# A two-layer encoder trunk: the pre-norm root moved to the product's eviction, the residual taken through PSUM chunk by chunk, and the other half's steps placed in the chains at a fixed pace

## Chip, cores and metric

The kernel runs on one NeuronCore of a Trainium2 chip. The metric is the device time of one execution in microseconds: three runs gave 1231.95, 1235.25 and 1236.02 us, median 1235.25 us. The trace quoted below comes from one further execution under the hardware profiler, which took 1234.75 us.

## What is computed

The reference is a trunk of two layers on one sequence of 512 positions with 1024 channels, in float32. Every sub-layer is a sandwich of two RMS norms around a function f:

```python
def rms_norm(x, g):
    y = x * lax.rsqrt(jnp.mean(x * x, axis=-1, keepdims=True) + EPS)
    return y * g

for i in range(2):
    g = sandwich_gains[i]
    h = rms_norm(x, g[0])
    m = parallel_conv_mla(h, ...) if i == 0 else conformer_conv(h, ...)
    x = x + rms_norm(m, g[1])
    h = rms_norm(x, g[2])
    x = x + rms_norm(jnp.square(jax.nn.relu(h @ w1[i])) @ w2[i], g[3])
```

Layer 0's mixer is a gated short convolution beside latent attention, followed by one output projection (`wout`). Layer 1's mixer is a Conformer module: a projection to 2048 columns (`pw1`) with a GLU (a times the sigmoid of g), a depthwise convolution of 31 taps, a LayerNorm over the channels, SiLU, and a projection (`pw2`). The MLP has 4096 hidden columns.

What matters for the change is that an RMS norm is a gain per channel times one factor per position, the reciprocal root of the mean square. The factor is the same for all channels of a position, so it can be applied to `h` before a matrix product or to the product's columns after it.

## The kernel before

**Layout.** Channels lie on the 128 partitions and positions along the free axis, so a 1024-channel activation is 8 tiles, called chunks here (`xs`, `ms`, `hs`). Every float32 operand of a matrix product is split into a high and a low part, and a product is three matmuls (`mm`, lines 252 to 254): high by high, high by low, low by high. A step is one output block of 128 channels over 8 input chunks, 24 matmuls. ScalarE (ACT) writes the high half as a rounded copy, VectorE (DVE) or GpSimd (POOL) subtracts it to get the low half (`split`, lines 236, 239 and 242). Weights come in by DMA in strips, are split in the same way (`strip`, lines 228 to 230) and are prepared some strips ahead (`take`).

**Halves and steps.** The positions are worked in two halves, A and B, each 256 wide (240 and 272 in layer 1). `M0`, `M2` and `M3` list tokens, and `run` turns them into steps. The tokens `up`, `down`, `pw1`, `pw2` and `wout` are products: eight steps to a group. `up` is a block of `w1` with the squared ReLU (written to `hid`); `down` is a block of `w2`, added to `m`; `pw1` makes two products and the GLU, and then starts the convolution of that channel chunk. The tokens `join`, `norm` and `finish` are chains: work on one half that PE can do little for.

**The chains.** A `join` ends one sub-layer and prepares the next: `residual` takes the reciprocal root of the mean square of `m` (`rstds`: a sum over partitions with matmuls at line 345, a Newton iteration of twelve small DVE operations at lines 376 to 407, and a spreading matmul at line 417), multiplies each chunk of `m` by it (446) and adds it, with the gain, to `x` in place (439). `prenorm` squares the new `x` chunk by chunk on ACT (336), adds the squares on DVE (323), takes the second root in the same way, and then makes each chunk of `h` = x times gain times root (465) and its two halves (236, 239). Only then can the next product of that half begin. `norm` is the LayerNorm of the Conformer module (`layer_norm`, 818 to 831). `finish` writes the output.

**What sets the order.** In `M2` and `M3` the DVE instructions run in the order in which the program emits them (`manual_schedule`); the scheduler orders the other engines by its own estimates, and in `M0` DVE too. Each engine's queue is in order. While a half is in a chain, `pull(i)` at fixed places of the chain emits some of the following steps of the other half; how many is listed by hand for each chain in `PULLS`, or else in `PULL`. So for `join A 1 1` the tuple (2, 2, 0, 0, 9) means two steps before the first root, two after it, none before and after the squares, and nine after the second root.

**The convolution.** Its 31 taps a chunk are DVE operations on a PSUM bank (786), emitted between the product steps: each step grants a number of microseconds (`FILL`), and one tap is emitted for every 0.4 us (`TAP_US`). `norm` first emits the taps that are left.

**PSUM.** There are eight banks: three `S`, two `pj`, one `o`, two `mi`. Products take `S` and `pj` in turn, but `S` alone while convolutions, which live in `pj`, are open (`accum`). Scratch tiles of the chains take `o` and `mi`.

**An up step's eviction** is `y` = Relu of the product on ACT (480), its square on ACT (482), or on DVE for the four tokens in `SQ` (484), the high half on ACT (236) and the low half on DVE (242).

Of the kernel before, what the change touches and what calls it, by code (L numbers as in the profile page):

```python
# [42 lines left out]
FILL = {'up': 2.2, 'down': 3.2, 'first': 2.7, 'sum': 0, 'pw1': 3.9, 'pw2': 2.8, 'last': 5.1, 'wout': 1.5}  # L43
# [17 lines left out]
CHAIN = {"sq": 3, "acc1": 2, "t": 2, "t2": 2}  # L61
# [73 lines left out]
def trunk(ctx: ExitStack, tc: tile.TileContext, a, out: bass.AP):  # L135
# [15 lines left out]
    def phase(name, acc, **tags):  # L151

        pool = tc.tile_pool(name=name, bufs=1, reuse_waits="tile")
        scope.update(name=name, sb=pool.__enter__(), tags=tags, acc=acc, turn=0, scr=0, scratch=["o", "mi"], raws=0, los=0, lo=(1, 0), sum=nc.vector)
        return pool
# [19 lines left out]
    def scratch(w):  # L177


        scope["scr"] += 1  # L180
        return ps(scope["scratch"][scope["scr"] % len(scope["scratch"])])[:, :w]
# [115 lines left out]
    def pull(i):  # L297

        scope["pulling"] = True
        n = scope["pulls"][i]  # L300
        while n and steps and not steps[0][0] and steps[0][1][1] not in ("F", scope["half"]):
            steps.pop(0)[2]()
            n -= 1
        scope["pulling"] = False
# [127 lines left out]
    def residual(xs, ms, s, gain, seg):  # L432

        pull(0)
        bc = rstds(s, "post")
        pull(1)

        def add(j, t):
            nc.vector.scalar_tensor_tensor(
                out=xs[j][seg.sl], in0=t, scalar=col(gain + j), in1=xs[j][seg.sl],  # L440
                op0=ALU.mult, op1=ALU.add,
            )

        for j in range(NC):
            t = scratch(seg.w)
            nc.vector.tensor_tensor(out=t, in0=ms[j][seg.sl], in1=bc, op=ALU.mult)
            settle()
            late.append(lambda j=j, t=t: add(j, t))
        settle()

    def prenorm(xs, gain, hs, seg):

        hs = views(hs, seg)
        s = Sum(NC, seg, whole=WHOLE[0])
        pull(2)
        for j in range(NC):
            s.square(xs[j][seg.sl])
            settle(1)
        settle()
        pull(3)  # L460
        bc = rstds(s, "pre")
        pull(4)
        for j in range(NC):
            t = scratch(seg.w)
            nc.vector.scalar_tensor_tensor(
                out=t, in0=xs[j][seg.sl], scalar=col(gain + j), in1=bc, op0=ALU.mult, op1=ALU.mult
            )
            settle()
            split((hs[j][0][seg.sl], hs[j][1][seg.sl]), t, nc.vector, late=late)
        settle()  # L470
# [4 lines left out]
    def up(w, hs, dst, seg):  # L475
# [4 lines left out]
        nc.scalar.activation(y, acc, AF.Relu)  # L480
        if scope["square"] is nc.scalar:
            nc.scalar.activation(acc, y, AF.Square)
        else:
            nc.vector.scalar_tensor_tensor(
                out=acc, in0=acc, scalar=0.0, in1=y, op0=ALU.max, op1=ALU.mult
            )
        split((dst[0][cols], dst[1][cols]), acc, nc.vector)
# [266 lines left out]
    def glu(c, wa, wg, seg):  # L754
# [3 lines left out]
        tg = tmp("sg")[:, : seg.w]  # L758
        nc.scalar.activation(tg, accg, AF.Sigmoid, bias=col(V_BPW1 + NC + c))
# [33 lines left out]
    def layer_norm(seg):  # L793
# [15 lines left out]
        pull(0)  # L809
        s2 = Sum(NC, seg, whole=WHOLE[2])  # L810
        for c in range(NC):
# [8 lines left out]
            s2.square(v)  # L820
        settle()
        pull(1)
        rb = rstds(s2, "var")
        pull(2)
        for c in range(NC):
# [5 lines left out]
            split((hv[c][0][seg.sl], hv[c][1][seg.sl]), t, nc.vector, late=late)  # L831
        settle()
# [10 lines left out]
    hid, sums, kept, us = {}, {}, {}, []  # L843
# [4 lines left out]
    def up_step(tok, h, layer, g, m):  # L848
# [3 lines left out]
        scope["square"] = nc.vector if tok[:4] in SQ else nc.scalar  # L852
        up(take(), hs, hid[h][m], seg)
        fill(FILL["up"])

    def down_step(tok, h, layer, g, m):
        last = g == G - 1
        if last and m == 0:
            sums[h] = Sum(NC, seg_of(h, layer), whole=WHOLE[4])
# [15 lines left out]
    def pw1_step(tok, h, c):  # L875
        seg = seg_of(h, 0)
        glu(c, take(), take(), seg)
# [22 lines left out]
    def join_step(tok, h, layer, n):  # L900
        seg = seg_of(h, layer)
        residual(xs, ms, sums[h], gains(layer, n), seg)
        prenorm(xs, gains(layer, 2) if n == 1 else gains(layer + 1, 0), hs, seg)

    def finish_step(tok, h):
        seg = seg_of(h, 1)
        pull(0)
        bc = rstds(sums[h], "finish")
        pull(1)
# [12 lines left out]
        for j in (*pool, *(j for j in range(NC) if j not in pool)):  # L922
# [5 lines left out]
            late.append(lambda j=j, x=x, t=t: add(j, x, t))  # L928
        settle()

    def run(program, in_order=True):
# [38 lines left out]
        with order:  # L970
            while steps:
                chain, tok, fn = steps.pop(0)
                if chain:
# [138 lines left out]
```

## Time and profile before

| | |
|---|---|
| median of three runs | 1235.25 us |
| the profiled execution's own time | 1234.75 us |
| its span, first to last instruction | 1232.9 us |
| mean granted clock of TensorE | 0.977 |
| weights and inputs read from HBM | 180.42 MB, 148 GB/s over the span |
| share of the chain that ended last | PE 81%, DVE 12%, ACT 3% |

The time lies 1.85 us above the span. Some first readings: the page gives each engine's busy time with its share of the span and its number of instructions, then 40 slices of 30.8 us each, one digit a slice, in tenths. PE's busy time is modelled: matmuls overlap, so a matmul of 256 columns shows as 0.28 us although the next one starts 0.12 us later. Counts in a window tell more than busy time. A line "X <- Y: a, b, c" in the list of waits means that X waited for Y for a us in all, b times, c us at the longest. A row of a timeline has the start in us, the duration in us, the engine, the line of the kernel and the tiles; a wait before it stands in brackets at its end.

### The profile page before, as it was taken

The page shows a single profiled execution, that of the slowest core. Times are in us where ns is not written, and L with a number is a line of the kernel's source. Part 1 is how long each engine was busy: PE and PEld are TensorE (multiplying, and loading weights), DVE is VectorE, ACT ScalarE, POOL GpSimd, SP SyncE. Part 2 cuts the span into 40 slices and gives each one's busy share as a digit, 9 for nine tenths or more (in the row PEclk, how much of TensorE's full clock was granted, in tenths as well). Part 3 has the DMA queues.
Part 4 walks back from the last instruction along what each step waited for, and adds up shares of the span by engine and source line. Part 5 has one row for each costly group of instructions (what it writes and reads, how often), then busy time and mean ns, then how long its engine had stood idle before and what let it go on. Part 6 is the DMA issues. An engine that isn't in the chain of part 4 may idle for free.

```text
span 1232.9 us, 22940 instructions
## 1 busy us (share of the span) xinstructions
PE 1176.0 (95%) x8926; PEld 1131.6 (92%) x8926; DVE 706.3 (57%) x1667; ACT 660.0 (54%) x1174; POOL 787.6 (64%) x388
## 2 busy tenths in 40 slices
PE   6999989999999999999999989999999889999996
PEld 3788869989999999899999989999999889999996
DVE  7843599555254235678965547498995354261313
ACT  4421577455555556546466746564455756445462
POOL 5564563145857777688874644688886665748680
PEclk9999999999999999999998989899999899999998
DMA  6331232044644565455543524655552652636341
GB/s 202 110 100 35 90 112 69 1 154 138 226 155 137 206 231 184 149 185 190 180 160 127 202 90 171 206 189 188 171 173 85 222 171 86 217 124 222 124 152 37
DMA packets 55405, 184.01 MB, mean 149 GB/s; under 512 B 6400, under 2 KB 10880, under 8 KB 55296
## 3 DMA queue, kind: packets, MB, share of 16 engines
q1 hardware_dynamic: 54864, 182.00, 44.1%
q8 instruction: 70, 1.15, 0.4%
q10 hardware_dynamic: 432, 0.54, 0.1%
q14 instruction: 39, 0.32, 0.1%
HBM read 180.42 MB, written 2.10 MB: 148 GB/s over the span
## 4 chain that ended last, share of the span: by engine, by line
PE 81%; DVE 12%; ACT 3%; issue 1%; DMA 1%; POOL 0%; SPq 0%; DVEq 0%; ACTq 0%
PE S L252 17%; PE S L253 17%; PE S L254 17%; PE pj L252 8%; PE pj L253 8%; PE pj L254 8%; DVE pj L786 4%; PE mi L345 1%; PE mi L417 1%; ACT whi L229 1%; DVE ycat L323 1%; DVE pr L721 1%; DVE h L535 1%; PE mi L724 1%; DVE s L715 1%
## 5 line engine op out<-in xcount | busy, mean ns | idle before, releaser
L230 POOL TENSOR_TENSOR wlo<-raw,whi 128x1024 fp32r<-128x1024 f32 (+3 forms) x316 | 738.1, 2350 | 374.9 <-ACT whi L229 348.9
L229 ACT ACTIVATE whi<-raw 128x1024 fp32r<-128x1024 f32 (+2 forms) x347 | 355.7, 1031 | 408.2 <-PE S L253 169.9
L252 PE MATMUL S<-h,whi 128*128 128x256 f32 (+2 forms) x1120 | 328.7, 295 | 8.9 <-ACT h L236 3.9
L253 PE MATMUL S<-h,whi 128*128 128x256 f32 (+2 forms) x1120 | 328.9, 294 | 0.1
L254 PE MATMUL S<-h,wlo 128*128 128x256 f32 (+2 forms) x1120 | 327.6, 293 | 0.0
L252 PEld LDWEIGHTS S<-h,whi 128*128 128x128 f32 x1120 | 213.1, 191 | 15.0 <-ACT h L236 4.7
L253 PEld LDWEIGHTS S<-h,whi 128*128 128x128 f32 x1120 | 213.6, 191 | 4.9 <-DVE h L239 1.3
L254 PEld LDWEIGHTS S<-h,wlo 128*128 128x128 f32 x1120 | 213.8, 191 | 3.6
L254 PE MATMUL S<-hid,wlo 128*128 128x256 f32 (+1 forms) x680 | 194.4, 286 | 0.0
L253 PE MATMUL S<-hid,whi 128*128 128x256 f32 (+1 forms) x680 | 194.0, 286 | 0.0
L786 DVE SCALAR_TENSOR_TENSOR pj<-u,taps,pj 128x240 f32<-128x240 f32 (+1 forms) x464 | 192.4, 489 | 1.1
L252 PE MATMUL S<-hid,whi 128*128 128x256 f32 (+1 forms) x680 | 192.4, 285 | 0.5 <-DVE m L494 0.5
L252 PE MATMUL pj<-h,whi 128*128 128x256 f32 (+2 forms) x432 | 132.6, 307 | 10.6 <-ACT whi L229 4.8
L253 PE MATMUL pj<-h,whi 128*128 128x256 f32 (+2 forms) x432 | 132.5, 307 | 2.6 <-DVE h L536 2.6
L254 PE MATMUL pj<-h,wlo 128*128 128x256 f32 (+2 forms) x432 | 130.6, 302 | 0.0
L252 PEld LDWEIGHTS S<-hid,whi 128*128 128x128 f32 x680 | 129.7, 191 | 0.8 <-DVE m L494 0.7
L254 PEld LDWEIGHTS S<-hid,wlo 128*128 128x128 f32 x680 | 130.2, 192 | 0.1
L253 PEld LDWEIGHTS S<-hid,whi 128*128 128x128 f32 x680 | 129.9, 191 | 0.0
L253 PE MATMUL pj<-hid,whi 128*128 128x256 f32 (+1 forms) x344 | 100.4, 292 | 0.0
L254 PE MATMUL pj<-hid,wlo 128*128 128x256 f32 (+1 forms) x344 | 99.7, 290 | 0.0
L252 PE MATMUL pj<-hid,whi 128*128 128x256 f32 (+1 forms) x344 | 98.9, 289 | 0.0
L252 PEld LDWEIGHTS pj<-h,whi 128*128 128x128 f32 x432 | 82.5, 191 | 16.2 <-ACT whi L229 7.6
(214 smaller groups left out, 1854.7 us busy)
## 6 DMA issues: line engine op xcount, KB each, us to landing
raw<-in_w SPq DMA_DIRECT2D x256, 512.0 KB, 3.8
raw<-in_pw SPq DMA_DIRECT2D x48, 512.0 KB, 3.6
raw<-in_win SPq DMA_DIRECT2D x16, 512.0 KB, 3.4
x<-in_xT SPq DMA_DIRECT2D x16, 256.0 KB, 4.2
raw<-in_wout SPq DMA_DIRECT2D x8, 512.0 KB, 3.4
raw<-in_wq SPq DMA_DIRECT2D x8, 192.0 KB, 2.3
out<-x SPq DMA_DIRECT2D x8, 120.0 KB, 1.7
out<-x SPq DMA_DIRECT2D x6, 136.0 KB, 1.8
```

The source lines that it names most:

```text
L229: nc.scalar.activation(h, r, AF.Copy)
L230: eng.tensor_tensor(out=lo[:, c0:c1], in0=r, in1=h.bitcast(F32), op=ALU.subtract)
L252: nc.tensor.matmul(acc, sh, mh, start=i == 0, stop=False)
L253: nc.tensor.matmul(acc, sh, ml, start=False, stop=False)
L254: nc.tensor.matmul(acc, sl, mh, start=False, stop=i == n - 1)
L323: self.eng.tensor_tensor(out=dst, in0=acc, in1=t, op=ALU.add)
L345: nc.tensor.matmul(s[:bw, b : b + 1], q[:, cols], one, start=i == 0, stop=i == len(self.parts) - 1,)
L417: nc.tensor.matmul(o[:, sl], r[:, b : b + 1].to_broadcast([bw, P]), ident[:bw, :bw], start=True, stop=True,)
L535: nc.vector.tensor_scalar(out=hi, in0=x, scalar1=g, scalar2=None, op0=ALU.mult)
L715: nc.vector.reduce_max(out=mx, in_=S, axis=AX.X)
L721: eng.tensor_scalar(out=pr_, in0=pr_, scalar1=sm, scalar2=None, op0=ALU.mult)
L786: nc.vector.scalar_tensor_tensor(out=dst, in0=src, scalar=wk, in1=acc, op0=ALU.mult, op1=ALU.add)
```

## The change

Five things are edited together.

- `join` replaces `residual` and `prenorm`. After the first root, a loop over the chunks makes three things per chunk, one turn apart: the product with the root into a PSUM scratch tile, the new residual into another PSUM scratch tile, and from that the two halves of `h` = x times gain (without a root) and the copy of the residual back to `x` on ACT. Then come the squares, the second root, and a copy of its spread to a tile `bcs` of its own for each half.
- `up` and `glu` apply that root where the product is evicted: `up` on DVE, as max(product, 0) times root, in place of the Relu on ACT, with the square always on ACT and the low half emitted one step later; `glu` by two more DVE operations per step. `SQ` goes.
- `pull` and its tables go. `pace(us)` adds an estimated time and emits one step of the other half whenever 2.9 us have gathered.
- In a chain, the steps that are emitted take `S` banks alone, and scratch tiles turn through `o`, `pj`, `mi`, `pj`.
- `FILL` for `up` falls from 2.2 to 1.9 us.

```diff
-PULLS = {('join', 'B', 0, 1): (3, 8, 4, 4, 7), ('join', 'A', 0, 1): (0, 0, 1, 4, 2), ('finish', 'B'): (0, 31), ('join', 'B', 0, 3): (1, 5, 0, 5, 5), ('norm', 'B'): (0, 2, 2), ('finish', 'A'): (3, 4), ('join', 'A', 0, 3): (0, 2, 1, 3, 5), ('norm', 'A'): (0, 0, 5), ('join', 'A', 1, 1): (2, 2, 0, 0, 9), ('join', 'B', 1, 1): (0, 1, 0, 3, 1)}
-PULL = {'join': (0, 1, 2, 0, 1), 'norm': (0, 2, 1), 'finish': (0, 2)}
-SQ = {('up', 'B', 1, 0): 1, ('up', 'A', 0, 2): 1, ('up', 'A', 0, 0): 1, ('up', 'B', 1, 1): 1}
+STEP_US, EDGE_US, ROOT_US, CHUNK_US, SQUARE_US = 2.9, 1.0, 2.8, 1.45, 0.5
...
-FILL = {'up': 2.2, 'down': 3.2, 'first': 2.7, 'sum': 0, 'pw1': 3.9, 'pw2': 2.8, 'last': 5.1, 'wout': 1.5}
+FILL = {'up': 1.9, 'down': 3.2, 'first': 2.7, 'sum': 0, 'pw1': 3.9, 'pw2': 2.8, 'last': 5.1, 'wout': 1.5}
...
-        tags = [t for t in scope["acc"] if t != "pj" or not (convs or todo)]
+        tags = [t for t in scope["acc"] if t != "pj" or not (convs or todo or scope.get("chain"))]
...
+        tags = ["o", "pj", "mi", "pj"] if scope.get("chain") else ["o", "mi"]
+        return ps(tags[scope["scr"] % len(tags)])[:, :w]
...
+    def pace(us):
+        scope["time"] += us
+        while scope["time"] >= STEP_US and steps and not steps[0][0] and steps[0][1][1] not in ("F", scope["half"]):
+            scope["time"] -= STEP_US
+            scope["pulling"] = True
             steps.pop(0)[2]()
+            scope["pulling"] = False
+        scope["time"] = min(scope["time"], STEP_US)
...
+    def join(xs, ms, s, post, pre, hs, seg, h):
+        hv = views(hs, seg)
+        pace(EDGE_US)
         bc = rstds(s, "post")
+        pace(EDGE_US + ROOT_US)
+        ts, xn = {}, {}
+        for j in range(NC + 2):
+            if j < NC:
+                ts[j] = scratch(seg.w)
+                nc.vector.tensor_tensor(out=ts[j], in0=ms[j][seg.sl], in1=bc, op=ALU.mult)
+            if 1 <= j <= NC:
+                i = j - 1
+                xn[i] = scratch(seg.w)
+                nc.vector.scalar_tensor_tensor(
+                    out=xn[i], in0=ts[i], scalar=col(post + i), in1=xs[i][seg.sl], op0=ALU.mult, op1=ALU.add
+                )
+                nc.scalar.activation(hv[i][0][seg.sl], xn[i], AF.Copy, scale=col(pre + i))
+                nc.scalar.activation(xs[i][seg.sl], xn[i], AF.Copy)
+            if j >= 2:
+                i = j - 2
+                nc.vector.scalar_tensor_tensor(
+                    out=hv[i][1][seg.sl], in0=xn[i], scalar=col(pre + i), in1=hv[i][0][seg.sl].bitcast(F32),
+                    op0=ALU.mult, op1=ALU.subtract,
+                )
+            pace(CHUNK_US)
+        ssq = Sum(NC, seg, whole=WHOLE[0])
         for j in range(NC):
+            ssq.square(xs[j][seg.sl])
+            settle(1)
+            pace(SQUARE_US)
         settle()
+        pace(EDGE_US)
+        bc = rstds(ssq, "pre")
+        bcs[h] = tmp("bcs" + h)
+        if seg.n > seg.w:
+            nc.gpsimd.memset(bcs[h][:, seg.w : seg.n], 0.0)
+        nc.scalar.activation(bcs[h][:, : seg.w], bc, AF.Copy)
+        pace(ROOT_US)
...
-        nc.scalar.activation(y, acc, AF.Relu)
-        if scope["square"] is nc.scalar:
-            nc.scalar.activation(acc, y, AF.Square)
-        else:
-            nc.vector.scalar_tensor_tensor(
-                out=acc, in0=acc, scalar=0.0, in1=y, op0=ALU.max, op1=ALU.mult
-            )
-        split((dst[0][cols], dst[1][cols]), acc, nc.vector)
+        nc.vector.scalar_tensor_tensor(
+            out=y, in0=acc, scalar=0.0, in1=bc[:, : seg.n], op0=ALU.max, op1=ALU.mult
+        )
+        nc.scalar.activation(acc, y, AF.Square)
+        settle()
+        split((dst[0][cols], dst[1][cols]), acc, nc.vector, late=late)
...
+        for acc in (acca, accg):
+            nc.vector.tensor_tensor(out=acc, in0=acc, in1=bc[:, : seg.w], op=ALU.mult)
         nc.scalar.activation(tg, accg, AF.Sigmoid, bias=col(V_BPW1 + NC + c))
```

In `layer_norm` and `finish_step` each `pull` becomes a `pace`: for the LayerNorm `EDGE_US`, then `2 * SQUARE_US` after each of the eight squares, `EDGE_US`, `EDGE_US + ROOT_US`, and `2 * SQUARE_US` after each of the eight chunks of SiLU. The first step of a `down` group emits the low half that is still waiting.

More of the change, by code (lines that the diff above doesn't have):

```diff
@@ L155, in phase @@
         pool = tc.tile_pool(name=name, bufs=1, reuse_waits="tile")
-        scope.update(name=name, sb=pool.__enter__(), tags=tags, acc=acc, turn=0, scr=0, scratch=["o", "mi"], raws=0, los=0, lo=(1, 0), sum=nc.vector)
+        scope.update(name=name, sb=pool.__enter__(), tags=tags, acc=acc, turn=0, scr=0, raws=0, los=0, lo=(1, 0), sum=nc.vector)
         return pool
@@ L295, in trunk @@
     steps = []
[L297 to L301, printed above, removed]
+    def pace(us):
[3 more added lines that the diff above has]
+            scope["pulling"] = True
             steps.pop(0)[2]()
-            n -= 1
-        scope["pulling"] = False
+            scope["pulling"] = False
+        scope["time"] = min(scope["time"], STEP_US)
     class Sum:
@@ L444, in residual @@
         for j in range(NC):
[L445 to L448, printed above, removed]
+            ssq.square(xs[j][seg.sl])
+            settle(1)
+            pace(SQUARE_US)
         settle()
[L451 to L470, printed above, removed]
+        pace(EDGE_US)
@@ L808, in layer_norm @@
         fill(GAP)
-        pull(0)
+        pace(EDGE_US)
         s2 = Sum(NC, seg, whole=WHOLE[2])
@@ L820, in layer_norm @@
             s2.square(v)
+            pace(2 * SQUARE_US)
         settle()
-        pull(1)
+        pace(EDGE_US)
         rb = rstds(s2, "var")
-        pull(2)
+        pace(EDGE_US + ROOT_US)
         for c in range(NC):
@@ L831, in layer_norm @@
             split((hv[c][0][seg.sl], hv[c][1][seg.sl]), t, nc.vector, late=late)
+            pace(2 * SQUARE_US)
         settle()
@@ L840, in start @@
                 convolve(*todo.pop(0))
-    hid, sums, kept, us = {}, {}, {}, []
+    hid, sums, kept, us, bcs = {}, {}, {}, [], {}
     def seg_of(h, layer):
@@ L851, in up_step @@
             hid[h] = hids(seg.lo)
-        scope["square"] = nc.vector if tok[:4] in SQ else nc.scalar
-        up(take(), hs, hid[h][m], seg)
+        up(take(), hs, hid[h][m], seg, bcs[h])
         fill(FILL["up"])
@@ L857, in down_step @@
         last = g == G - 1
+        if m == 0:
+            settle()
         if last and m == 0:
@@ L876, in pw1_step @@
         seg = seg_of(h, 0)
-        glu(c, take(), take(), seg)
+        glu(c, take(), take(), seg, bcs[h])
         start(c, seg)
@@ L901, in join_step @@
         seg = seg_of(h, layer)
-        residual(xs, ms, sums[h], gains(layer, n), seg)
-        prenorm(xs, gains(layer, 2) if n == 1 else gains(layer + 1, 0), hs, seg)
+        pre = gains(layer, 2) if n == 1 else gains(layer + 1, 0)
+        join(xs, ms, sums[h], gains(layer, n), pre, hs, seg, h)
     def finish_step(tok, h):
         seg = seg_of(h, 1)
-        pull(0)
+        pace(EDGE_US)
         bc = rstds(sums[h], "finish")
-        pull(1)
+        pace(EDGE_US + ROOT_US)
         pool = POOL_OUT[h]
@@ L928, in finish_step @@
             late.append(lambda j=j, x=x, t=t: add(j, x, t))
+            pace(2 * SQUARE_US)
         settle()
@@ L972, in run @@
                 chain, tok, fn = steps.pop(0)
-                if chain:
-                    scope["half"], scope["pulls"] = tok[1], PULLS.get(tok, PULL[tok[0]])
+                scope["half"], scope["chain"], scope["time"] = tok[1], chain, 0.0
                 fn()
+                scope["chain"] = False
     run(M0, "M0" in IN_ORDER)
```

15 lines of the change are left out of this document (3 added, 12 removed).

## The prediction

> **What bounds the kernel now.** I read the page's head first, for how much of the span TensorE could still give back.
>
> ```profile
> span 1232.9 us, 22940 instructions
> ...
> PE 1176.0 (95%) x8926; PEld 1131.6 (92%) x8926; DVE 706.3 (57%) x1667; ACT 660.0 (54%) x1174; POOL 787.6 (64%) x388
> ...
> PEclk9999999999999999999998989899999899999998
> ```
>
> PE is the bound, and the change takes no matrix product away: what can be won is time in which PE stands still or runs at a lowered clock. The page spreads that thin, so I asked for windows around each place where the row of slices dips, PE alone. The last row is a stretch without a dip.
>
> ```profile
> 268.00:284.00 16.00, 12.94 (x88) 0.79 0.68 237
> 490.00:516.00 26.00, 23.04 (x178) 0.93 0.40 131
> 704.00:724.00 20.00, 16.08 (x115) 0.83 0.50 179
> 764.00:784.00 20.00, 18.23 (x130) 0.83 0.45 164
> 1006.00:1032.00 26.00, 21.70 (x161) 0.93 0.35 119
> 644.00:660.00 16.00, 13.59 (x94) 0.79 0.30 97
> 955.00:975.00 20.00, 15.92 (x94) 0.83 0.69 245
> 868.00:884.00 16.00, 14.32 (x115) 1.00 0.52 165
> 375.00:464.00 89.00, 88.81 (x750) 1.00 0.56 190
> ```
>
> Columns: stretch, its length, PE busy, matmuls, granted clock. Busy time hides the loss; counts show it. The last row gives 89.00 / 750 = 0.1187 us a matmul, so one step of 24 matmuls is 2.85 us. Length less count times 0.1187 is the loss: 5.6 us at 268 (join A 0 1), 4.9 at 490 (join A 0 3 and the first pw1), 6.4 at 704 (join A 1 1), 4.6 at 764 (join B 0 3), 6.9 at 1006 (join B 1 1): 28.2 us at five joins. The two LayerNorms (norm A at 644, norm B at 955) lose 4.8 and 8.8, a place in convolution B 2.4. Join B 0 1 shows no dip. The clock column splits it: 0.79 of 16 us is 3.4 us gone to the clock, 0.93 of 26 us 1.8; over the five joins 3.4 + 1.8 + 3.4 + 3.4 + 1.8 = 13.8 us, about half.
>
> Then the waits of PE, and the timeline of one join, A 1 1, engine by engine (PE, ACT, DVE).
>
> ```profile
> PE mi L417 <- DVE s L407: 9.2, 4, 2.4
> PE mi L345 <- DVE acc L323: 8.8, 4, 4.0
> ```
>
> ```profile
> 710.70 0.28 PE L252 MATMUL S<-hid,whi 128*128 128x256 f32 x1
> 712.49 0.34 PE L345 MATMUL mi<-kst,acc 128*120 128x1 f32 x2 [1.51 <-DVE acc L323]
> ...
> 715.87 1.18 PE L417 MATMUL mi<-kst,s 120*128 120x120 f32 x4 [2.41 <-DVE s L407]
> 716.72 0.56 PE L253 MATMUL S<-hid,whi 128*128 128x256 f32 x1
> ```
>
> ```profile
> 712.38 0.38 ACT L236 ACTIVATE hid<-S 128x256 fp32r<-128x256 f32 x1
> ```
>
> ```profile
> 715.57 0.16 DVE L407 SCALAR_TENSOR_TENSOR s<-mi,s 120x2 f32<-120x2 f32 x1
> 715.64 0.41 DVE L242 TENSOR_TENSOR hid<-pj,hid 128x256 fp32r<-128x256 f32 x1
> 715.97 0.41 DVE L242 TENSOR_TENSOR hid<-S,hid 128x256 fp32r<-128x256 f32 x1
> ```
>
> The waits name the sum and the root of the chain, but PE still had eight down steps of B to do. At 710.70 it starts one of them and stops: the low halves of `hid` (L242) are missing. ACT finished their high halves by 712.76; DVE, whose order is written by hand, reaches the subtractions at 715.64, right behind the last operation of the root (L407), because `PULLS` gives this join no step between its squares and the second root. So the loss is not a lack of work for PE. It is the other half's evictions queued on DVE behind the chain, and then the lowered clock.
>
> **The joins.** Removed: `PULLS`, and the second root from the path to the next product: `h` is now x times gain, ready chunk by chunk, and the root multiplies the product. Added: a step of the other half whenever the chain's estimated time has grown by 2.9 us, close to the 2.85 measured. A join's estimates sum to 1.0 + 3.8 + 10 x 1.45 + 8 x 0.5 + 1.0 + 2.8 = 27.1 us, nine steps, 25.7 us of PE; eight or more of the other half stand behind each of the five joins.
>
> ```profile
> L439 DVE SCALAR_TENSOR_TENSOR x<-mi,vec,x 128x256 f32<-128x256 f32 x16 | 7.6, 478 | 0.0
> ...
> L446 DVE TENSOR_TENSOR mi<-m,mi 128x256 f32<-128x256 f32 x16 | 6.8, 426 | 2.5 <-PE mi L417 2.2
> ...
> L239 DVE TENSOR_TENSOR h<-mi,h 128x256 fp32r<-128x256 f32 x16 | 6.7, 421 | 4.2 <-ACT h L236 4.1
> ...
> L484 DVE SCALAR_TENSOR_TENSOR S<-S,y 128x256 f32<-128x256 f32 x9 | 3.8, 424 | 1.5 <-ACT y L480 1.5
> ```
>
> ```profile
> L236 ACT ACTIVATE hid<-S 128x256 fp32r<-128x256 f32 x71 | 27.1, 383 | 7.9 <-DVE S L484 6.3
> L480 ACT ACTIVATE y<-S 128x256 f32<-128x256 f32 x71 | 26.0, 366 | 1.9 <-PE S L254 1.9
> L482 ACT ACTIVATE S<-y 128x256 f32<-128x256 f32 x62 | 24.0, 388 | 1.7
> ```
>
> (The last two columns of a group are busy time, mean ns of one, and idle time before it.) A chunk costs DVE the product with the root (0.43), the residual (0.48) and the low half, now a scalar_tensor_tensor (bounded by 0.42 and 0.48): 1.3 to 1.4 us, so ten turns of the loop take 13 to 14, and the five steps within them about 0.85 each (0.42 for the relu-and-root, 0.42 for the low half), 4.2 more: 17 to 18 us for 14.3 us of PE. DVE is a little slower than the pace there. With 2.2 us of root (twelve small operations of 0.16 and their gaps, as at L407) and the matmuls about it, some 5 us, the last chunk is there about 23 us after the sum, when PE has just spent eight steps (22.8 us). The squares and the second root follow under the remaining steps and under the first products, which fill up to five banks (14 us) before one of them has to be evicted. On ACT two copies of 0.38 a chunk are added and the Relu (0.37 x 128 steps = 47 us) goes; the 32 squares that `SQ` gave DVE come back (12 us). None of that is on the path.
>
> So the joins' 28.2 us should go, but not all: I leave one wait of the kind quoted, 2.4 us and the 3.4 us of clock that follow it, 5.8 us in the five together. **Joins: -22.4 us** (bounds -28.2, if none is left, and -12, if two of five stay as they are).
>
> [...]
>
> **The convolution stretches.** Here DVE has least to spare.
>
> ```profile
> 510.00:630.00 120.00, 119.55 (x992) 119.12 (x993) 105.80 (x276) 63.18 (x98) 105.46 (x49) 0.99 0.58 189
> 562.60:608.20 45.60, 45.60 (x388) 45.60 (x387) 41.52 (x111) 25.52 (x41) 39.84 (x20) 1.00 0.55 180
> 790.00:935.00 145.00, 143.16 (x1201) 142.22 (x1200) 122.05 (x296) 74.18 (x112) 122.65 (x56) 1.00 0.56 180
> 860.00:888.00 28.00, 26.32 (x216) 25.59 (x215) 28.00 (x71) 9.78 (x10) 22.99 (x11) 1.00 0.53 170
> 1035.00:1200.00 165.00, 165.00 (x1315) 164.91 (x1314) 46.68 (x97) 85.25 (x140) 115.51 (x49) 1.00 0.49 166
> ```
>
> (Busy PE, PEld, DVE, ACT, POOL, each with its count.) Per operation DVE takes 41.52 / 111 = 0.374 us in convolution A and 28.00 / 71 = 0.394 in B. Added in each half: two products with the root in each of 8 pw1 steps and one operation in each of 16 up steps, 32 x 0.374 = 12.0 us and 32 x 0.394 = 12.6. Free: 120 - 105.8 = 14.2 and 145 - 122.05 = 22.9. It fits on the whole, not everywhere: a down step brings 3.2 / 0.4 = 8 taps and an addition, 9 x 0.374 = 3.4 us against 2.85, a backlog of 4.1 us in eight steps (5.6 in B). `FILL` for up falls from 2.2 to 1.9, so an up step has 4.75 taps and two operations, 2.52 us in A and 2.66 in B, where it had 2.43 and 2.56: it regains less. And with `pj` taken by the convolutions, PE has three banks; the low half, which frees one, is now emitted one step later, so PE can lead by about 2 us less. I let 1.5 us of this reach PE in A and 4.5 in B: **+6 us** (bounds 0, all in free time, and 24.6, none).
>
> **The norms.** The same pace frees their evictions, seven steps by the estimates; 4.8 us at norm A end with a wait for the root as above. Against that the up steps' smaller share leaves 16 x 0.3 / 0.4 = 12 taps for later, 4.5 to 4.7 us of DVE ahead of each norm, while the PE steps that cover it stay eight. **0 us** (-9 to +9).
>
> **The rest.** In 1035 to 1200 PE is busy without a gap and DVE 28%: an added 0.42 a step (less 0.42 where `SQ` stood) is hidden; uncovered it would be 0.42 us at each change from up to down, 16 times, 6.7 us. The tail after the last product is not touched. **0 us.**
>
> Sum: -22.4 + 6 + 0 + 0 = -16.4 us on the profiled run's own 1234.75 us gives 1218.4; the median of the three, 1235.25, is 0.5 above that run, so 1218.5 for the median.
>
> **Rivals.**
> - *DVE becomes the bound in the convolutions (slower).* Place: up and pw1 steps between the taps. Price: all 24.6 us reach PE, and both norms start late by 4.5 us more; with the joins at -22.4 that is +11, about 1246. It decides once three banks leave PE no lead over DVE. For it: 28.00 of 28.00 us busy at 860. Against: 22.9 us free around it. 0.13.
> - *The pace hides, but pulled steps hold the chain.* A pulled step's first DVE operation waits for PE, and the chain stands behind it; the join's PE order, which the scheduler estimates, may also put its matmuls late. Then half of the joins' loss stays: -12 + 6 = -6, 1229. For it: at 17 to 18 us against 14.3, DVE is already over the pace. 0.17.
> - *It changes nothing measurable:* joins -12 meet convolutions +12: 1235. 0.08.
> - *More:* no wait left at joins (-28.2), norms -8, convolutions +2: -34, 1201. For it: the norms' waits are of the kind removed. 0.17.
>
> My forecast has 0.45. **Numbers.** 0.3% is 3.7 us, about what a measurement of this kernel can tell. Faster by more: forecast, "more", and most of the second rival, 0.77; within: 0.09; slower: 0.14. The range, 1199 to 1241, leaves out the slower rival's far half and gains beyond the joins and norms together.
>
> **What would show it.** Right: the windows of the five joins at about 0.1187 us a matmul with a clock of 1.0; L242 subtractions between the chunks of the chain; PE's waits for L407 and L345 down from 18 us to under 6. DVE busy in the convolutions above 92%, with gaps in PE near the change from down to up. Wrong: joins still with a clock under 0.9; or a stretch of PE waiting for DVE within the taps for more than 10 us in all.

## The result, and the profile after

Six runs of the changed kernel gave 1241.77 to 1249.43 us, median 1247.24; six of the kernel before on the same chip 1231.95 to 1236.96, median 1235.15. The ratio is 1.0099, 95% interval [1.0073, 1.0124]: slower by 1%, where 16.4 us less, 1.3%, was forecast. The profiled execution of the changed kernel took 1242.59 us.

The lines move: the spreading matmul is now L419, the sum matmul L347, the last operation of a root L409, the adds of squares L325, the low half of `hid` L239 (emitted late), `up`'s product with the root L485, its square L488, the GLU's products with the root L763 and its sigmoid L764. First the page's head:

```profile
span 1240.8 us, 22874 instructions
...
PE 1169.6 (94%) x8926; PEld 1122.0 (90%) x8926; DVE 729.0 (59%) x1747; ACT 645.9 (52%) x1132; POOL 795.9 (64%) x389
...
PEclk9999999999999999999999899999999899999998
```

The same 8926 matmuls; DVE has 22.7 us more, ACT 14.1 less. Now windows of PE alone, in the columns of the first window table of the prediction, at the same work (it comes at other times):

```profile
268.00:284.00 16.00, 16.00 (x139) 1.00 0.73 247
464.00:512.00 48.00, 44.36 (x365) 1.00 0.49 164
604.00:628.00 24.00, 21.02 (x164) 0.93 0.47 151
640.00:664.00 24.00, 21.67 (x173) 1.00 0.20 67
684.00:712.00 28.00, 22.44 (x158) 0.88 0.46 168
744.00:772.00 28.00, 23.08 (x175) 0.94 0.31 115
796.00:930.00 134.00, 120.34 (x993) 1.00 0.53 169
960.00:985.00 25.00, 19.84 (x143) 0.86 0.49 174
1000.00:1034.00 34.00, 32.26 (x269) 1.00 0.53 174
1035.00:1200.00 165.00, 165.00 (x1327) 1.00 0.50 165
```

At 0.1187 us a matmul, join A 0 1 (268) now loses nothing and join B 1 1 (1000) 2.1 us, but join A 1 1 (684) loses 9.2, and join B 0 3 (744) 7.2. Join A 0 3 (464) is at full clock and still loses 4.7 (4.9 before). Convolution B (796) lost 2.4 us before and now loses 134.00 - 993 x 0.1187 = 16.1; the end of convolution A (604) loses 4.5. The norms (640, 960) lose 3.5 and 8.0. The waits of PE, four lines out of the list:

```profile
PE S L252 <- DVE hid L239: 18.7, 12, 3.7
PE S L252 <- ACT y L764: 10.1, 7, 1.4
...
PE mi L419 <- DVE s L409: 2.3, 1, 2.3
...
PE mi L347 <- DVE acc L325: 1.5, 1, 1.5
```

The 18.0 us of waits for a root or a sum have fallen to 3.8. In their place PE waits for a free `S` bank: for the late low half of `hid` and for the GLU's sigmoid.

Since all 8926 matmuls are there on both sides, I read a third thing from the traces: the time at which the n-th matmul starts, stretch by stretch, less the same time in the kernel before (us, one profiled run each; the last four columns are experiments told below).

| matmuls | place | after | e9 | e7 | e14 | e15 |
|---|---|---|---|---|---|---|
| 1300 to 1600 | join A 0 1 | -6.4 | -6.3 | -6.3 | -6.3 | -6.4 |
| 3000 to 3500 | join A 0 3, first pw1 | -0.1 | -1.9 | -1.9 | -1.9 | +9.5 |
| 4200 to 4400 | end of convolution A | +4.0 | +0.1 | +0.1 | +0.4 | +6.6 |
| 4400 to 4700 | norm A | -0.9 | +2.7 | +1.5 | +3.3 | +1.7 |
| 4700 to 5200 | join A 1 1 | +3.4 | +1.0 | -5.3 | -5.4 | +3.8 |
| 5200 to 5600 | join B 0 3 | +2.5 | -3.3 | -3.4 | -4.2 | +6.8 |
| 5600 to 6800 | convolution B | +13.7 | +4.9 | +4.9 | +4.9 | +37.7 |
| 6800 to 7100 | norm B | +0.2 | -3.8 | -5.6 | -5.3 | +1.4 |
| 7100 to 7600 | join B 1 1 | -5.1 | -4.9 | -4.9 | -4.9 | -5.0 |
| sum of the five joins | | -5.7 | -15.4 | -21.8 | -22.7 | +8.7 |
| both convolutions | | +17.7 | +5.0 | +5.0 | +5.3 | +44.3 |

In the changed kernel the joins give 5.7 us back instead of 22.4, the convolutions take 17.7 instead of 6, the norms -0.7 instead of 0, and all the rest -3.0: +8.3.

Each column is one execution, and that limits what it can tell. The changed kernel's lies 4.65 us below its median, so 8.3 of the 12.1 us between the medians are placed here. e7's lies 8.3 below its median and e14's 3.7; the kernel before's 1234.75 is 4 to 5 us above its medians beside the experiments (1229.7 to 1230.93). So a difference of some 5 us between two columns counts only where the medians bear it out.

What such a wait is made of, in join A 1 1 of the changed kernel. The timeline of PE (only the row with the wait), of ACT, and of DVE:

```profile
692.79 0.38 PE L252 MATMUL S<-h,whi 128*128 128x256 f32 x1 [2.93 <-DVE hid L239]
```

```profile
691.48 0.39 ACT L488 ACTIVATE S<-y 128x256 f32<-128x256 f32 x1 [3.91 <-DVE y L485]
691.90 0.38 ACT L236 ACTIVATE hid<-S 128x256 fp32r<-128x256 f32 x1
```

```profile
688.33 0.16 DVE L409 SCALAR_TENSOR_TENSOR s<-mi,s 120x2 f32<-120x2 f32 x1
688.41 2.70 DVE L230 TENSOR_TENSOR wlo<-raw,whi 128x1024 fp32r<-128x1024 f32 x1
691.03 0.41 DVE L485 SCALAR_TENSOR_TENSOR y<-S,bcsB 128x256 f32<-128x256 f32 x1
691.37 0.40 DVE L447 TENSOR_TENSOR pj<-m,mi 128x240 f32<-128x240 f32 x1
691.68 0.41 DVE L485 SCALAR_TENSOR_TENSOR y<-S,bcsB 128x256 f32<-128x256 f32 x1
692.32 0.42 DVE L239 TENSOR_TENSOR hid<-S,hid 128x256 fp32r<-128x256 f32 x1 [0.23 <-ACT hid L236]
```

Read from the bottom of DVE's rows: the bank that PE wants is free after L239 at 692.32. L239 needs ACT's high half (691.90), this the square (691.48), this `y`, which is DVE's own L485 at 691.03. L485 stood behind a root and a 2.70 us subtraction of weights. ACT waited 3.91 us for it. Before, the Relu, the square and the high half ran on ACT without DVE (but for the four tokens in `SQ`), and only the low half came to DVE's queue: one place per step. Now a step has two, with ACT between them. The path itself has hardly grown: DVE's 0.41 us stand where ACT's Relu takes 0.36 (e14 below).

### The profile page after: what moved, and what is told of

It is laid out like the page before. It is cut to its first block, busy times and chain, and to the rows that moved or that the text cites. A ratio compares the mean times of both kernels' runs of the same rounds, so it can differ in the third digit from the quotient of the medians.

```text
span 1240.8 us, 22874 instructions
## 1 busy us (share of the span) xinstructions
PE 1169.6 (94%) x8926; PEld 1122.0 (90%) x8926; DVE 729.0 (59%) x1747; ACT 645.9 (52%) x1132; POOL 795.9 (64%) x389
## 5 line engine op out<-in xcount | busy, mean ns | idle before, releaser
L252 PE MATMUL S<-h,whi 128*128 128x256 f32 (+2 forms) x1224 | 362.2, 297 | 36.4 <-DVE hid L239 18.7
L253 PE MATMUL S<-h,whi 128*128 128x256 f32 (+2 forms) x1224 | 359.9, 294 | 0.2
L254 PE MATMUL S<-h,wlo 128*128 128x256 f32 (+2 forms) x1224 | 359.0, 293 | 0.0
L252 PEld LDWEIGHTS S<-h,whi 128*128 128x128 f32 x1224 | 235.3, 192 | 46.5 <-DVE hid L239 21.0
L253 PEld LDWEIGHTS S<-h,whi 128*128 128x128 f32 x1224 | 235.6, 192 | 4.3 <-DVE h L239 0.8
L252 PE MATMUL S<-hid,whi 128*128 128x256 f32 (+1 forms) x784 | 220.3, 283 | 3.7 <-DVE acc L325 1.7
L253 PE MATMUL S<-hid,whi 128*128 128x256 f32 (+1 forms) x784 | 221.0, 283 | 0.2
L252 PEld LDWEIGHTS S<-hid,whi 128*128 128x128 f32 x784 | 146.8, 188 | 5.3 <-PE S L254 2.3
L253 PEld LDWEIGHTS S<-hid,whi 128*128 128x128 f32 x784 | 147.2, 188 | 0.8 <-DVE hid L239 0.8
L252 PE MATMUL pj<-h,whi 128*128 128x256 f32 (+2 forms) x328 | 102.0, 311 | 8.8 <-ACT whi L229 4.7
L253 PE MATMUL pj<-h,whi 128*128 128x256 f32 (+2 forms) x328 | 102.1, 311 | 2.6 <-DVE h L539 2.6
L254 PE MATMUL pj<-h,wlo 128*128 128x256 f32 (+2 forms) x328 | 100.8, 307 | 0.0
L252 PEld LDWEIGHTS pj<-h,whi 128*128 128x128 f32 x328 | 62.1, 189 | 13.9 <-ACT whi L229 6.9
L253 PEld LDWEIGHTS pj<-h,whi 128*128 128x128 f32 x328 | 62.2, 190 | 7.6 <-DVE h L539 4.9
L254 PE MATMUL pj<-hid,wlo 128*128 128x256 f32 (+1 forms) x240 | 68.4, 285 | 0.0
L253 PE MATMUL pj<-hid,whi 128*128 128x256 f32 (+1 forms) x240 | 68.0, 283 | 0.0
```

Of the source, the lines that this page charges most:

```text
L252: nc.tensor.matmul(acc, sh, mh, start=i == 0, stop=False)
L253: nc.tensor.matmul(acc, sh, ml, start=False, stop=False)
L254: nc.tensor.matmul(acc, sl, mh, start=False, stop=i == n - 1)
```

## The experiments

The theory that I came to is this: a pulled step's eviction now has **two places in DVE's in-order queue**, and whatever stands in front of the first one delays the whole eviction, and with it a bank (in the rows above a root and 2.70 us of weights in front, ACT's wait of 3.91 us, PE's of 2.93). The main rival is **DVE's time**: more DVE operations where DVE has none to spare. All ratios are to the kernel before, timed on the same chip.

**Weight subtractions taken off DVE (e1, e13).** `LO` says how many of so many strips have their low half subtracted on DVE; (1, 0) is none.

```diff
-('up', 'A', 1, 0): (5, 2), ('down', 'A', 0, 0): (2, 1), ('up', 'A', 1, 3): (4, 1), ('up', 'B', 0, 3): (3, 1)
+('up', 'A', 1, 0): (1, 0), ('down', 'A', 0, 0): (1, 0), ('up', 'A', 1, 3): (1, 0), ('up', 'B', 0, 3): (1, 0)
```

> The changed kernel with one table edited: the low halves of the weights of the four step groups that are pulled into chains (up B 0 3, up A 1 0, up A 1 3, down A 0 0) all go to POOL, none to DVE. Queue theory (in a chain, products have three banks, and one comes free only when DVE, in the order of the chain, reaches the low half of an earlier pulled step): each weight subtraction of 1.2 to 2.7 us on DVE within joins A 1 1 and B 0 3 delays that, so the two joins lose 4 to 8 us less together, 1247 becomes 1239 to 1243. Cover theory (the chain is longer than the work that the other half has for PE, and PE waits for h): the chain gets shorter only by what DVE did of the weights, 2 us at most, 1245 to 1247. POOL theory (POOL then becomes late with the weights): slower than 1247.

> The kernel before, with only the table of low halves changed: no weight subtractions on DVE in the up steps that stand in or behind the joins (the same edit that took 0.7% from the changed kernel). Nothing is left out. Theory: in the kernel before a step's eviction visits DVE once and PE waits in the joins for the chain's order, not for weights; so little changes: 0.996 to 1.002. Rival: these subtractions cost the kernel before as much as the changed one; then 0.991 to 0.994, and the gain of the edit belongs to no part of the change.

The changed kernel with this edit (e1) came to 1.0026 [1.0002, 1.0049], the kernel before with it (e13) to 0.9987 [0.9976, 0.9998]. So by the medians the subtractions cost the changed kernel 0.7% and the other 0.1%. (The one profiled execution of e13 is 5.1 us shorter at join B 0 3 than that of the kernel before, and 6.5 in all, more than its medians bear out.) In e1 the place is the one shown above: join A 1 1 goes from +3.4 to -3.7, join B 0 3 from +2.5 to -1.1, and the convolutions stay at +17.7: that part of the loss has another cause.

**The residual kept in SBUF (e2).** This lets the pulled steps have `pj` again and saves the copy back on ACT.

```diff
-                xn[i] = scratch(seg.w)
+                xn[i] = xs[i][seg.sl]
...
-                nc.scalar.activation(xs[i][seg.sl], xn[i], AF.Copy)
```

> The changed kernel with the new residual written straight into x in SBUF, as in the kernel before, and the two halves of h made from there; the copy back goes, and so both lines on PSUM banks are undone: pulled steps may take pj again, scratch tiles take o and mi. Queue theory: with five banks instead of three PE can run ahead over the chain; joins A 0 3, A 1 1 and B 0 3 get back 3 to 5 us each, 1247 becomes 1233 to 1238. Cover theory: banks are not short, the joins stay as they are, 1245 to 1249. A third: a low half with both inputs in SBUF is slower beside POOL and the chain grows, over 1249.

It came to 1.0211 [1.0188, 1.0235], as its third expectation had it, and says nothing on the banks, since another cost came in: the chunk's low half now has both inputs in SBUF. One line of its groups, against 478 ns with one input in PSUM, and two of its timelines, DVE's and POOL's:

```profile
L457 DVE SCALAR_TENSOR_TENSOR h<-x,vec,h 128x256 fp32r<-128x256 f32 x32 | 31.6, 992 | 3.7 <-ACT h L454 3.7
```

```profile
267.97 0.47 DVE L457 SCALAR_TENSOR_TENSOR h<-x,vec,h 128x256 fp32r<-128x256 f32 x1
269.81 1.83 DVE L457 SCALAR_TENSOR_TENSOR h<-x,vec,h 128x256 fp32r<-128x256 f32 x2
```

```profile
268.55 2.41 POOL L230 TENSOR_TENSOR wlo<-raw,whi 128x1024 fp32r<-128x1024 f32 x1 [3.69 <-ACT whi L229]
```

At 267.97, with POOL idle, it takes 0.47 us; at 269.81, with a subtraction of weights on POOL, the first of the two takes 1.43 (the row groups two). I come back to it at the end. What more banks in the chains would be worth was not measured; e14 below gets its joins with the same three.

**The GLU's root (e3, e4, e5).** In all three the GLU is without its root. In e3 nothing stands in its place; in e4 two spare DVE operations stand behind the release of the banks; in e5 the same with a PSUM operand.

```diff
-        for acc in (acca, accg):
-            nc.vector.tensor_tensor(out=acc, in0=acc, in1=bc[:, : seg.w], op=ALU.mult)
...
+        spare = ps("o")[:, : seg.w]
+        nc.vector.tensor_scalar(
+            out=spare, in0=u[:, HALO + seg.lo : HALO + seg.hi], scalar1=1.0, scalar2=0.0, op0=ALU.mult, op1=ALU.add
+        )
+        nc.vector.tensor_tensor(out=spare, in0=spare, in1=bc[:, : seg.w], op=ALU.mult)
```

(The removed lines are e3, both hunks e5; e4 has two products of `u` with `bc` into an SBUF tile instead.)

> The changed kernel without the root in the GLU: the two DVE products per pw1 step are left out, so that part of the computation is missing. Both theories of the convolution stretches expect a gain: 32 operations of 0.38 to 0.41 us, 12 to 13 us, if all of them reach PE: 1234 to 1237; if half do, 1241.

> As the run without the root in the GLU, but DVE does two products of the same width in each pw1 step, from SBUF into a spare SBUF tile, behind the operation that frees the product's bank: the same DVE work, not ahead of the sigmoid, and no bank held for it (the root is missing from the GLU here too). Bank theory (what costs is that the two products stand between PE and the release of its three banks): nearly the gain of the run without them, 1234 to 1239. Throughput theory (DVE has no time left in the convolution stretches): no gain, 1244 to 1248.

> Repeats the run with the two products moved, without its flaw: there both inputs lay in SBUF, and one operation took 1.26 to 1.44 us instead of 0.43. Here the GLU again lacks the root, and behind the operation that frees the product's bank DVE does two operations with one operand in PSUM (the free bank o), 0.53 and 0.43 us. Bank theory: as the run without the root in the GLU, 0.2% under the kernel before to 0.3% over it. Throughput theory (DVE is full in the convolution stretches, wherever the work stands): as the changed kernel, 0.8 to 1.2% over the kernel before.

e3 0.9982 [0.9967, 0.9997]; e4 1.0209 [1.0182, 1.0236]; e5 1.0060 [1.0032, 1.0088]. e3's gain, 1.2%, is a little more than the 12 to 13 us given. e4 is spoilt like e2: its spare products, both inputs in SBUF, took 1436 and 1264 ns where the GLU's own, with one in PSUM, take 427. Between e5 and the others: taking the products out of the way of the banks, with as many operations on DVE, is a third of what the GLU's root costs (1.0099 to 1.0060), leaving them out is the rest (to 0.9982). So e5 lies between its two expectations, and for the GLU DVE's time is not excluded. A wait of PE there, in convolution B of the changed kernel, with DVE and ACT:

```profile
853.60 0.39 PE L252 MATMUL S<-h,whi 128*128 128x256 f32 x1 [1.44 <-ACT y L764]
```

```profile
852.20 0.43 DVE L763 TENSOR_TENSOR S<-S,bcsB 128x256 f32<-128x256 f32 x1 [1.43 <-PE S L254]
853.58 0.48 DVE L768 SCALAR_TENSOR_TENSOR u<-S,vec,y 128x256 f32<-128x256 f32 x1 [0.95 <-ACT y L764]
```

```profile
852.13 1.06 ACT L229 ACTIVATE whi<-raw 128x1024 fp32r<-128x1024 f32 x1 [1.77 <-PE S L253]
853.10 0.46 ACT L764 ACTIVATE y<-S,vec 128x256 f32<-128x256 f32 x1
```

DVE waits for PE (1.43) and multiplies until 852.63; but ACT copies a strip of weights until 853.19, and the sigmoid comes behind that. So here PE waits for ACT's queue, and not for the product. All seven waits of this kind in the changed kernel look the same. Without a product in front of the sigmoid three are left in e3, and three in e5, each as long (1.44):

```profile
PE S L252 <- ACT y L762: 4.3, 3, 1.4
```

The root thus makes these waits more frequent (10.1 us in seven), and not longer; by which way it does so was not tried.

**Pending low halves at once (e6, e15).** If the second visit only comes too late, it should help to make it earlier: e6 (on e1) puts a `settle()` at the head of each turn of the join's loop, e15 (on e1) emits `up`'s low half at once.

```diff
-        settle()
-        split((dst[0][cols], dst[1][cols]), acc, nc.vector, late=late)
+        split((dst[0][cols], dst[1][cols]), acc, nc.vector)
```

> The changed kernel with the weights of the pulled steps on POOL (as in the first run of this series), and one line more: at the head of each turn of the chunk loop the low half that waits is emitted, so that a pulled step's bank is free one chunk (1.3 us) after its root operation rather than at the next pulled step, two chunks on. Queue theory: join A 0 3, which still loses about 5 us, and B 0 3 get back 2 to 3 us each, 4 to 6 us less than that first run (0.26% over the kernel before becomes 0.1 to 0.25% under). Cover theory: no change, or 1 to 2 us more because DVE waits for the high half within the chain.

> The changed kernel without weight subtractions on DVE in the pulled up steps (1.0026), with up's low half emitted at once and not one step later. Nothing is left out. Theory (two visits): DVE then waits within each step for ACT's square and high half, some 1 us, and whatever stands behind it on DVE waits too, so it is no better and rather worse: 1.002 to 1.015. Rival (the deferral holds the bank one step longer, and PE stands for that): 0.990 to 0.998.

e6 1.0296 [1.0242, 1.0349], e15 1.0509 [1.0481, 1.0538]. I had first thought of the order alone, and e6 was to cure it; that fell. DVE then waits in place for ACT's square and high half (for the high half of `hid` 34.7 us in e1, 185.1 in e15), and everything behind it waits too: PE's waits for the low half of `hid` go from 15.8 us in e1 to 31.2 in e6, and e15 has 50.1 us of PE's time there in 32 waits.

```profile
PE S L252 <- DVE hid L242: 50.1, 32, 3.5
```

So the sign is the theory's, its size three times what I gave it (1.002 to 1.015). Deferring the low half, a part of the change, is what keeps its other part from costing 5%.

**`up` evicted as before (e9, e7).** Relu and square on ACT, one visit of DVE; the second root is then missing in the MLP's hidden layer. It is a factor per position, and the post-norm behind the MLP divides it out again, up to `EPS`.

```diff
-        nc.vector.scalar_tensor_tensor(
-            out=y, in0=acc, scalar=0.0, in1=bc[:, : seg.n], op0=ALU.max, op1=ALU.mult
-        )
+        nc.scalar.activation(y, acc, AF.Relu)
         nc.scalar.activation(acc, y, AF.Square)
-        settle()
-        split((dst[0][cols], dst[1][cols]), acc, nc.vector, late=late)
+        split((dst[0][cols], dst[1][cols]), acc, nc.vector)
```

> The changed kernel with one part undone: up is evicted as before (Relu and square on ACT, low half on DVE at once), the table of low halves as in the changed kernel. The second root is left out of the MLP's hidden layer (a factor per position, which the post-norm behind the MLP divides out again). Theory: up's root on DVE makes each pulled step visit the DVE queue twice, with ACT in between, and long subtractions of weights in that queue hurt only because of the two visits. Then this alone brings nearly what the two edits together brought (0.9897): 0.990 to 0.995, and the waits of PE for the low half of hid within the joins fall below 4 us. Rival: the weight subtractions cost their 0.7% by themselves, whoever evicts; then 0.997 or more, with the loss still in join A 1 1.

> The changed kernel with the weights of the pulled steps on POOL, and the up step's eviction as in the kernel before: Relu and square on ACT, the low half at once; the root is left out of the MLP's hidden layer. DVE saves 128 operations of 0.42 us, 32 of them in the convolution stretches, and PE's banks come free one step earlier there. If the up steps' share of the convolution loss is what the run without the root in the GLU left (about 6 us in B and 4 in A), this run is 8 to 11 us under that first run, 0.4 to 0.65% under the kernel before. If the share is only the DVE time (16 operations of 0.4 us a half, and FILL's 12 taps a half already given back), 3 to 5 us.

e9, this edit alone: 0.9909 [0.9889, 0.9929]. e7, with e1's edit: 0.9897 [0.9852, 0.9942], below the 0.9935 to 0.996 that I gave it. The edit turns 1% slower into 0.9% faster. My clause that the weight subtractions hurt only because of the two visits does not hold in the trace: in e9's join A 1 1 PE still waits behind them, 6.0 us of the waits of this window, and the stretch goes from +1.0 in e9 to -5.3 in e7. Behind the root and a subtraction of 2.68 us the wait is 1.64 us there, where it was 2.93 with two places. The medians can't tell e9 and e7 apart, and e7's profiled execution was the fastest of its four by 7.4 us.

```profile
PE S L252 <- DVE hid L242: 6.0, 3, 2.9
```

**Place or time (e14).** e7 with the removed DVE operation put back, its result unused, right behind the low half: as much DVE work as in e1, but one place in the queue.

```diff
         split((dst[0][cols], dst[1][cols]), acc, nc.vector)
+        nc.vector.scalar_tensor_tensor(
+            out=y, in0=acc, scalar=0.0, in1=bc[:, : seg.n], op0=ALU.max, op1=ALU.mult
+        )
```

> The kernel of ratio 0.9897 (Relu and square on ACT, low half on DVE at once, no weight subtractions on DVE in pulled up steps), with an extra DVE operation in each up step: the same product of the bank with the root, max(bank, 0) times root, whose result nobody uses, right behind the low half. So DVE does as many and as long operations as in the kernel of ratio 1.0026 with up's root on DVE, but a step has one place in DVE's queue. The root is left out of the MLP's hidden layer. Theory (two visits): most of the gain stays, a part is lost in the convolutions where DVE has least to spare: 0.990 to 0.996. Rival (time on DVE): the gain goes, 1.000 to 1.005.

0.9897 [0.9843, 0.9951], the same as e7; the loss that I expected in the convolutions did not come (+5.3 beside +5.0). DVE has 707.1 us of work in it and 708.0 in e1, which came to 1.0026. So for `up` the 128 operations cost nothing measurable as time (the interval is 0.5% to either side); their place does. One of their groups, 51 of the 128, and PE's windows at the same work:

```profile
L488 DVE SCALAR_TENSOR_TENSOR y<-S,bcsA 128x256 f32<-128x256 f32 x51 | 21.1, 413 | 0.0
```

```profile
676.00:704.00 28.00, 28.00 (x238) 1.00 0.65 209
737.00:764.00 27.00, 26.60 (x226) 1.00 0.22 80
790.00:922.00 132.00, 125.97 (x1052) 1.00 0.53 181
```

Against 684:712, 744:772 and 796:930 above: joins A 1 1 and B 0 3 run without a loss (28.00 / 238 = 0.118, 27.00 / 226 = 0.119 us a matmul) at full clock, convolution B loses 132.00 - 1052 x 0.1187 = 7.1 us. And in the timeline of join A 1 1, ACT is done before DVE comes:

```profile
687.89 0.36 ACT L485 ACTIVATE y<-S 128x256 f32<-128x256 f32 x1
688.28 0.39 ACT L486 ACTIVATE S<-y 128x256 f32<-128x256 f32 x1
688.70 0.39 ACT L236 ACTIVATE hid<-S 128x256 fp32r<-128x256 f32 x1
```

```profile
690.59 0.42 DVE L242 TENSOR_TENSOR hid<-S,hid 128x256 fp32r<-128x256 f32 x1
690.92 0.41 DVE L488 SCALAR_TENSOR_TENSOR y<-S,bcsB 128x256 f32<-128x256 f32 x1
```

**Towards a better version (e8, e10, e11, e12).** e8 (on e1) and e10 (on e7) make the two joins ahead of `pw1` as before the change, at the new pace and with the root in `h`, so that the GLU needs none. e11 (on e7) leaves out squares and second root in the joins ahead of `up`, where nothing uses them any more. e12 is e10 and e11 together.

```diff
-        join(xs, ms, sums[h], gains(layer, n), pre, hs, seg, h)
+        if (layer, n) == (0, 3):
+            scope["chain"] = False
+            join_old(xs, ms, sums[h], gains(layer, n), pre, hs, seg)
+        else:
+            join(xs, ms, sums[h], gains(layer, n), pre, hs, seg, h, root=False)
```

> A complete kernel: the changed one with the weights of the pulled steps on POOL, in which the two joins ahead of pw1 (A 0 3 and B 0 3) are done as in the kernel before, with the root in h, but paced by estimated time; so the GLU needs no root, and these two chains let pulled steps use pj. If the 14 us that the root in the GLU costs come back and the two joins lose no more than now, 0.7 to 1.0% under the kernel before (1219 to 1222 beside 1231). If the longer chain costs PE 4 us at each, 0 to 0.3% under.

> The changed kernel with up evicted as before (root left out of the MLP's hidden layer), no weight subtractions on DVE in the pulled up steps, and the two joins ahead of pw1 as before the change (root in h, chain through x in place) at the new pace, so that the GLU needs no root. Theory: the GLU's two DVE operations cost about 9 us in the convolutions whatever up does, and an old-style join costs about 5 us more than a new one; so about 1 us either way around 0.9897: 0.985 to 0.993. Rival: the old-style joins lost in the earlier hybrid only because of up's two visits; then the convolutions' gain stays whole: 0.980 to 0.983.

> The kernel of ratio 0.9897 (up evicted as before, no weight subtractions on DVE in pulled up steps), and besides the joins ahead of up leave out their squares and second root altogether, since nothing uses them there (the root is left out of the MLP's hidden layer); the GLU keeps its root. Theory: with up freed of the root, squares and second root stand on no path of PE, so that leaving them out changes little: 0.986 to 0.991. Rival: the second root's small DVE operations and its two PE matmuls still hold the pulled steps; then 8 us more are gained, 0.983 or less, at joins A 1 1 and B 1 1.

> Put together: up evicted as before, no weight subtractions on DVE in pulled up steps, the joins ahead of up without squares and second root (the root is left out of the MLP's hidden layer), the two joins ahead of pw1 as before the change with the root in h, so that the GLU needs none. Theory: the parts' gains add up only in so far as they lie in different places; against 0.9876 (without the squares' removal) it gains what that brought elsewhere, 0.3%: 0.982 to 0.988. Rival: the squares' removal brought nothing beyond the scatter: 0.987 to 0.991.

e8 1.0062 [1.0034, 1.0090], outside both ranges given: with `up`'s two visits the joins of the old kind lose more (A 0 3 +7.6, B 0 3 +3.6). e10 0.9876 [0.9836, 0.9916]; e11 0.9864 [0.9821, 0.9908]; e12 0.9799 [0.9749, 0.9849], 1205.14 us against 1230.93, four runs from 1200.97 to 1214.68: faster than the kernel before by 2.0%. e10 lies in the theory's range; its convolutions come to -0.7 us, so what is left of them in e7, +5.0, is the GLU's root, and its joins ahead of `pw1` give most of that back (A 0 3 +0.2, not -1.9; B 0 3 +1.0, not -3.4). e11's interval holds both theories. e12's median lies below both ranges that were given for it, its interval reaches into the first. In all of e10 to e12 PE stands once at about 310 us, in the second chain, at the spreading matmul and waits for its root: 6.0 us in e10, 9.4 in the others, which e7 does not show. Why was not tried; it is what these three could still gain.

## Why the prediction was wrong

**The joins, -22.4 forecast, -5.7 measured: the step that failed.** The prediction costed `up`'s new eviction by duration: "the five steps within them about 0.85 each (0.42 for the relu-and-root, 0.42 for the low half)", added to DVE's busy time and found bearable. The durations are right (418 ns each), and e14 shows that so much DVE time is bearable: with it in one place the joins give -22.7. What it did not ask is where in DVE's order the 0.42 stands. Moved ahead of ACT's two operations, it made all three wait for whatever DVE was at: the chain's root, its chunks, a 2.70 us subtraction of weights. The step also counted nowhere the weight subtractions that pulled steps bring to DVE. Of the 16.7 us that were missing, one visit alone (e9) gives back 9.7, the subtractions taken off alone (e1: joins -16.3) 10.6, both (e7) 16.1. So in the joins it is the two together, and these single executions don't divide them; the medians give the subtractions 0.7% with two visits and nothing clear of noise with one.

**The convolutions, +6 forecast, +17.7 measured.** The same step is wrong here: with `up` in one place they come to +5.0 (e9) and +5.3 (e14), so some 12.5 us are `up`'s two visits, now among the taps; the late low half, which the prediction named, is part of them. The +5.0 is the GLU's root, for without it too (e10, where `FILL` is as low) they come to -0.7: DVE's backlog and `FILL`, the other costs named there, show no cost of their own. The forecast had the GLU's two products as 0.374 to 0.394 us each on DVE. Left out of the changed kernel they are worth 8.2 us of its convolutions (e3, +9.5), only moved 1.6 (e5, +16.1); how the larger part comes about stays open. So the forecast's +6 is near the +5.0 by luck: it was made of other terms.

**The norms, 0 forecast, -0.7 measured,** right, within -9 to +9.

**The rivals.** "DVE becomes the bound in the convolutions" gave 1246, within 1.3 us of what came, but by another mechanism: it kept the joins at -22.4. Nor does the trace show its premise, DVE full, where PE loses most. The two convolutions (PE, PEld, DVE, ACT, POOL), and two stretches of B:

```profile
512.00:628.00 116.00, 113.02 (x941) 112.61 (x940) 105.53 (x281) 55.34 (x81) 97.72 (x47) 0.99 0.55 177
796.00:930.00 134.00, 120.34 (x993) 117.75 (x992) 111.71 (x278) 58.55 (x82) 103.29 (x47) 1.00 0.53 169
850.00:870.00 20.00, 17.12 (x143) 16.71 (x142) 14.32 (x37) 6.57 (x9) 11.74 (x5) 1.00 0.36 126
870.00:890.00 20.00, 19.15 (x158) 18.60 (x158) 20.00 (x51) 7.14 (x7) 19.21 (x11) 1.00 0.62 194
```

DVE is busy 91% and 83%, less than the 92% that even the forecast expected. From 850 to 870 PE loses 20 - 143 x 0.1187 = 3.0 us with DVE busy for 14.32; from 870 to 890, where DVE is full, 1.2. What stays of this rival is the GLU, whose moved products (e5) still cost most of their price. "The pace hides, but pulled steps hold the chain" was nearest in kind, a pulled step standing badly in DVE's queue, but had it the wrong way round: here the chain, and the weights on DVE, hold the pulled step.

**What was to be seen.** Waits for the root and the sum under 6 us: 3.8, right. Join windows at full clock: right at A 0 1, A 0 3 and B 1 1, wrong at A 1 1 (0.88, under the 0.9 that was named as a sign of being wrong) and B 0 3 (0.94). Join windows at 0.1187 us a matmul: at A 0 1 alone; A 0 3 has 48.00 / 365 = 0.1315. Low halves between the chunks: there, but late. So the prediction's reading of the old loss was right (evictions queued on DVE behind the chain), and the change carried the same fault on: it moved more of the eviction onto the engine that was late. One reading was wrong without bearing on the sum: the change gives ACT one new copy a chunk, and not two, since the rounded copy stood in the kernel before; ACT's busy time fell by 14.1 us.

## What to carry to other kernels

Cost a moved operation by its place, not by its duration alone: list the engines that a tile passes on its way to freeing its buffer, and count how often it comes back to an in-order queue that also serves something long (here a root and 2.70 us of weights). One visit with two operations cost nothing measurable here (0.9897 in e14, and in e7 with one), two visits with one operation each cost 1.3% of the whole kernel (e1, 1.0026, against e14). Where a factor commutes with what follows, look whether something behind it divides it out before paying for it at every eviction.

## What the runs showed of the hardware

In e2, where both inputs of the low half of `h` lie in SBUF, its 48 operations on DVE took 0.45 to 2.52 us, median 0.49, 50.9 us in all. In the changed kernel, with one input in PSUM, the 48 took 0.45 to 0.50; the one from 262.39, 0.48 us, lies wholly within a subtraction of weights on POOL.

In e2's stretch from 262 to 273 us the long ones ended just after POOL did. The longest, 2.52 us from 262.63, ended at 265.15, and POOL's instruction at 264.86 (268.55 less the 3.69 us that POOL then sat idle), 0.29 us earlier. The one of 1.43 us from 269.81 ended at 271.24, and the subtraction on POOL, 2.41 us from 268.55, at 270.96, 0.28 us earlier. Between the two, with POOL idle, the operation took 0.47 us three times (265.40, 267.24, 267.97), and 0.47 as well at 271.89 beside memsets of 0.11 us each on POOL. What held the long ones up no trace shows.
